# Decay parameters in five background parts, sample chain and triangular inverse paced by the weights, cache rows and stores issued by SyncE

## The chip, the cores and the metric

The kernel runs on one core of a Trainium2 chip. TensorE (PE) multiplies, VectorE (DVE), ScalarE (ACT) and GpSimd (POOL) work on whole tiles, SyncE (SP) only issues transfers. SP's transfers run on a hardware queue (q1 in the profile), GpSimd's on a software queue (q0); both are carried by the same 16 DMA engines. The metric is the device time of one launch in microseconds. Before the change it is 2061.14 us, the median of three runs (2057.72 to 2062.92).

## The reference, cut to what matters

One layer of a decoder for 256 prompt tokens and 8 × 4 sample tokens (288 columns together), model width 2048:

```
h = RMSNorm(x)
(GDN q|k|v|z|beta|alpha, attention q|k|v (3 groups x 4 heads), pool channels, 3 gates) = h @ w_in
A: gated DeltaNet: short conv, SiLU, L2-normed q/k, per-head decay; prompt in chunks with the
   inverse of (1 + lower); sample from its own state
   beta = sigmoid(ba);  g = -exp(a_log) * softplus(aa + dt_bias);  decays from cumsum(g)
B: dilated window attention, groups (128,1), (512,4), (2048,16); sample tokens also see the caches
C: pooled channels, linear map
x = x + RMSNorm(merge(A, B, C with gates) @ w_out)
x = x + RMSNorm(SwiGLU(RMSNorm(x)))
```

The outputs also hold the new cache windows, GDN states, conv and pool rows. All is float32; a product of x and w is made of three products of rounded parts (wh·xh, wh·xl, wl·xh).

## The kernel before

**The main stream.** Some 590 weight tiles of 512 KB are read in a fixed order, one after another, and never again. SP loads a tile (`raw`, L169, five buffers), ACT rounds it (`wh`, L180), DVE subtracts (`wl`, L184), three buffers each, and PE runs 24 matmuls of 288 columns on it (L253 to L255). `plan` puts the items of the layer in a list (w_in by its column blocks, then the branch weights, w_out, the gate and up weights, w_down); `run_items` walks through it. At the end of an item its sums are taken out of PSUM (evacuations, `ev`).

**Background work.** Everything else is written as Python generators. After each tile `step` (L282) advances every started generator by its rate: R_G for the two head groups of the GDN (3.8 and 3.45 steps a tile), R_S = 4.4 for the sample attention, R_P = 1 for the prompt attention. A bare `yield` ends one step, `yield n` passes n tiles. The instructions are then put on their engines by a scheduler that estimates times; each engine runs its own in that order. `paced` (L274) puts an instruction behind the last `wl` on DVE, so that this work can't run ahead of the weights.

**GDN.** `beta_alpha` (L414) computes beta, the decays and their sums (`egc`, `egl`, `egls`) once, all in one piece, when two rounds of tokens are through. `gdn` (L662) does the prompt: the inverse of a triangular matrix takes 31 steps of two DVE instructions, `tm` (L741) and `X` (L743). `gdn_sample` (L854) has a chain of small matmuls with an engine's answer between: `ys`, `zs`, `ws`, `avs` (L891 to L912).

**Sample attention.** `attn_sample` (L1077) reads the caches as 118 rows `kr` of 256 KB (128 partitions × 512 values), in five buffers (KR = 5), keys first and values after. Groups 1 and 2 give 2 × 48 rows by L1106, whose source is four of the group's positions, each for 32 places (8 sequences × 4 quarters), thus 4 × 32 × 512; group 0 gives 2 × 8 by L1111 (128 × 512) and a few come from a scratch copy of the new rows (`scr`, L1089, L1112). DVE multiplies keys with queries (`junk`, L1142) and values with scores (`ot`, L1192). All these are issued by GpSimd (`dq = nc.gpsimd`). So are the stores of the new rows (`nat`, copied by L979 and L981): `win_prompt` (L986), `scr` (L988), `win_sample` (L991). Tiles like `nat`, `pT`, `oah`, `ev` and the GDN's are slots of one list of 98 (`U`, L123), handed out in the order in which they were freed: whoever takes a slot waits for the transfer that last read it.

Of the kernel before, what the change touches and what calls it, by code (L numbers as in the profile page):

```python
# [9 lines left out]
F32 = mybir.dt.float32  # L10
F32R = mybir.dt.float32r
AF = mybir.ActivationFunctionType
OP = mybir.AluOpType
# [4 lines left out]
NT, NP, NS = 288, 256, 32  # L18
# [6 lines left out]
KR = 5  # L25
EPS = 1e-6
SC = 128.0 ** -0.5
WIN = (128, 512, 1028)
# [59 lines left out]

class Layer:
    COPY_FROM = 310  # L90
    R_G, R_S, R_P, R_R = (3.8, 3.45), 4.4, 1, 1.4

    def __init__(self, ctx, tc, a, o):
        self.ctx, self.tc, self.nc, self.a, self.o = ctx, tc, tc.nc, a, o
        P = self.pool
        self.cp = P("cp")
        self.raw_p = P("rawp", 5)
        self.wh_p = P("whp", 3)
        self.wl_p = P("wlp", 3)
        self.up = P("up")  # L100
        self.sm = P("sm", 2)
        self.dr = P("dr", space=DRAM)
        self.pm = P("pm", 4, space=PSUM)
        self.pb = P("pb", 4, space=PSUM)
        self.ufree = deque(range(NU))
        self.uslot = {}
        self.bg = []
        self.chained = {}
        self.tiles = deque()
        self.pend = deque()  # L110
        self.items = []
        self.n = 0
        self.paced_to = None
        self.raws = deque()
        self.hold = None
        self.out_a, self.out_b, self.out_c = {}, {}, {}
        self.dq = self.nc.gpsimd
# [153 lines left out]
            self.behind(ins, self.chained[key])  # L271
        self.chained[key] = ins

    def paced(self, ins):  # L274

        if self.paced_to is not self.last_wl:
            self.paced_to = self.last_wl
            self.behind(ins, self.last_wl)
        self.chain(ins)
        return ins  # L280

    def step(self):  # L282
# [131 lines left out]
    def beta_alpha(self):  # L414
# [6 lines left out]
        for k in range(4):  # L421
            for j in range(4):
                d = j * 4 + k
                nc.tensor.matmul(p[32 * j:32 * j + 32, :NT], lhsT=w[:, d * 16:d * 16 + 32], rhs=self.xT[d],
                                 start=k == 0, stop=k == 3, tile_position=(0, 32 * j))
        bat = w
        nc.vector.tensor_tensor(bat, p[:, :NT], self.r0, op=OP.mult)
        pt = self.ps("bat")
        for ch in range(2):
# [1 line left out]
                             start=True, stop=True)  # L431
        nc.tensor.matmul(pt[:16, 32:64], lhsT=c["gsel"], rhs=bat[:, NP:], start=True, stop=True)
        nc.vector.tensor_copy(bat[:16, NP:], pt[:16, 32:64])
        dba = self.dr.tile([16, 32], F32, name="dba")
        self.dq.dma_start(dba, bat[:16, NP:])
        beta = self.cp.tile([128, 2, 9], F32, name="beta")
# [29 lines left out]
        nc.vector.tensor_tensor(w1, w1, w2, op=OP.add)  # L466
        nc.vector.scalar_tensor_tensor(w1, z2, 0.0, w1, op0=OP.max, op1=OP.add)
        nc.vector.scalar_tensor_tensor(g, w1, -1.0, ex[:, 2], op0=OP.mult, op1=OP.mult)
        pc = self.ps("cum")
        for k, (lu, lub) in enumerate((("U", "Ub"), ("V", "Vb"), ("ones", None))):  # L470
            nc.tensor.matmul(pc[:, k * 32:k * 32 + 18], lhsT=c[lu], rhs=g, start=True, stop=True)
# [8 lines left out]
                nc.scalar.activation(dst[:, :, 8:9], v[:, :, 8:9], AF.Exp)  # L480
        self.beta, self.gl, self.egc, self.esf, self.egl = beta, g, egc, esf, egl
        self.egls = []
        pe = self.ps("egls")
        for hg in range(2):
            t = self.cp.tile([128, 32], F32, name=f"egls{hg}")
            nc.vector.tensor_scalar(t, c["bsel"], g[:, hg * 9 + 8:hg * 9 + 9], None, op0=OP.mult)
            nc.tensor.matmul(pe[:, hg * 32:hg * 32 + 32], lhsT=c["ones"], rhs=t, start=True, stop=True)
            t2 = self.cp.tile([128, 32], F32, name=f"eglx{hg}")
            nc.scalar.activation(t2, pe[:, hg * 32:hg * 32 + 32], AF.Exp)
            self.egls.append(t2)  # L490


    def mixer_plan(self):
# [20 lines left out]

        def second():
            self.drain(self.rms0)
            self.beta_alpha()
            self.resc = self.start(self.rescale(), self.R_R)

        def conv_mixed():  # L520
# [64 lines left out]
                          after=(lambda blks=blks, part=part: self.down_done(blks, part)) if n == 3 else None)  # L585

    def gdn_start(self, hg):
        self.G[hg]["gen"] = self.start(self.gdn(hg), self.R_G[hg])

    def gdn_finish(self):  # L590
# [71 lines left out]
    def gdn(self, hg):  # L662
# [75 lines left out]
        for j in range(31):  # L738
            n, m = 31 - j, j + 1
            tv = tm[:, :n * m].rearrange("p (a b) -> p a b", a=n)  # L740
            nc.vector.tensor_tensor(tv, lb[:, j, j + 1:, None].to_broadcast([32, n, m]),  # L741
                                    X[:, j:j + 1, :m].to_broadcast([32, n, m]), op=OP.mult)
            nc.vector.tensor_tensor(X[:, j + 1:, :m], X[:, j + 1:, :m], tv, op=OP.subtract)  # L743
            yield
        nc.vector.tensor_copy(lb, X.rearrange("p i c -> p c i"))
# [108 lines left out]
    def gdn_sample(self, hg, G, la, kn, bv, beta, egc, nbe, kdc, qsc):  # L854
        nc, c, pp = self.nc, self.c, self.pap
        X = 8
# [31 lines left out]
        p = self.ps("ys")  # L888
        nc.tensor.matmul(p[:, 0:128], lhsT=x1[:, 0:128], rhs=R, start=True, stop=True)
        nc.scalar.copy(T[:, 0:128], p[:, 0:128])  # L890
        yield  # L891
        p = self.ps("zs")
        nc.tensor.matmul(p[:, 0:128], lhsT=x1[:, 128:256], rhs=T[:, 0:128], start=True, stop=True)
        nc.vector.tensor_copy(T[:, 128:256], p[:, 0:128])
        yield
        p = self.ps("ws")
        nc.tensor.matmul(p[:, 0:128], lhsT=x1[:, 0:128], rhs=T[:, 128:256], start=True, stop=True)
        V = T[:, 0:128]
        nc.vector.tensor_tensor(V, V, p[:, 0:128], op=OP.subtract)
        self.free(x1)  # L900
        yield
        p = self.ps("avs")
        nc.tensor.matmul(p[:, 0:128], lhsT=la[:, 128:256], rhs=V, start=True, stop=True)
        o = self.U(name="os")
        nc.vector.tensor_tensor(o[:, 0:128], qs, p[:, 0:128], op=OP.add)
        so = self.small(1, "sos")
        nc.scalar.activation(o[:, 128:256], o[:, 0:128], AF.Square, scale=qsc[:, X:X + 1], accum_out=so)
        nc.scalar.activation(so, so, AF.Sqrt, bias=self.eps, scale=1.0 / 128)
        nc.vector.reciprocal(so, so)
        nc.vector.tensor_tensor(so, so, qsc[:, X:X + 1], op=OP.mult)  # L910
        nc.scalar.activation(o[:, 0:128], o[:, 0:128], AF.Copy, scale=so)
        yield  # L912

        kd = kn[:, 0:128]
        nc.gpsimd.tensor_scalar(kd, kd, kdc[:, X:X + 1], None, op0=OP.mult)
# [39 lines left out]
    def evac_qkv(self, kind, g):  # L955
        vT = []

        def evac(h, ps):
            nc = self.nc
            t = self.res.popleft()  # L960
            nc.scalar.copy(t, ps)
            if kind == 2:
                vT.append(t)
            else:
                (self.kT if kind == 1 else self.qT)[g, h] = t
            if h < 3:
                return
            src = vT if kind == 2 else [(self.kT if kind == 1 else self.qT)[g, j] for j in range(4)]
            for tb in ([2] if kind == 0 else [1, 2] if (kind == 1 and g == 0) else [0, 1, 2]):
                w = NS if tb == 2 else 128  # L970
                p = self.ps("knat")
                for j in range(4):
                    nc.tensor.transpose(p[:w, j * 128:j * 128 + 128], src[j][:, tb * 128:tb * 128 + w],
                                        self.c["ident"])
                for hp in range(2):
                    n = self.U(name="nat")
                    cs = slice(hp * 256, hp * 256 + 256)
                    if hp == 0:
                        nc.scalar.copy(n[:w, :256], p[:w, cs])  # L979
                    else:  # L980
                        nc.vector.tensor_copy(n[:w, :256], p[:w, cs])  # L981
                    if tb < 2:
                        if not (g == 0 and tb == 0):
                            o = self.o[f"win{g + 1}_prompt"][0, 0].rearrange("r k h d -> r k (h d)")
                            r0 = 0 if g == 0 else tb * 128
                            self.dq.dma_start(o[r0:r0 + 128, kind - 1, cs], n[:, :256])  # L986
                    else:
                        self.dq.dma_start(self.scr[kind, g][:, cs], n[:NS, :256])  # L988
                        if kind > 0:
                            o = self.o[f"win{g + 1}_sample"][0].rearrange("b r k h d -> b r k (h d)")  # L990
                            self.dq.dma_start(o[:, WIN[g] - 4:, kind - 1, cs], n[:NS, :256])  # L991
                    if kind == 2 and tb < 2:
                        self.vn[g, tb, hp] = n
                    else:
                        self.free(n)
            self.free(*vT)
        evac.res = 4
        return evac
# [78 lines left out]
    def attn_sample(self, pool):  # L1077
# [8 lines left out]
        def by_t(dst, kind, g):  # L1086
            src = scr[kind, g].rearrange("(b t) d -> t b d", t=4)
            for t in range(4):
                dq.dma_start(dst[t * 32:t * 32 + 32], src[t][:, None, :].to_broadcast([8, 4, 512]))  # L1089

        for g in (1, 2):
            by_t(qt[:, g - 1], 0, g)
        q0s = scr[0, 0].rearrange("(b t) d -> t b d", t=4)
        for t in range(4):
            dq.dma_start(big[:, t], q0s[t][:, None, :].to_broadcast([8, 16, 512]))
        cw = [a["cache_win1"][0], a["cache_win2"][0], a["cache_win3"][0]]

        def row():
# [2 lines left out]
        def sources(kv):  # L1101

            for g, dil, n in ((1, 4, 32), (2, 16, 16)):
                src = cw[g].rearrange("b (q m r) k h d -> m k r (b q) (h d)", q=4, r=dil)
                for m in range(n):
                    yield g, (m if g == 1 else 32 + m), lambda kr, s=src[m, kv][:4]: dq.dma_start(kr, s)  # L1106
            for g in (1, 2):
                yield g, 47 + g, lambda kr, g=g: by_t(kr, 1 + kv, g)
            src = cw[0].rearrange("b (s m) k h d -> m k (b s) (h d)", m=8)
            for m in range(8):  # L1110
                yield 0, m, lambda kr, s=src[m, kv]: dq.dma_start(kr, s)  # L1111
            yield 0, 8, lambda kr: dq.dma_start(kr, scr[1 + kv, 0][:, None, :].to_broadcast([32, 4, 512]))  # L1112

        todo = deque((kv,) + r for kv in range(2) for r in sources(kv))
        got = deque()
# [13 lines left out]
                if not got:  # L1129
                    return  # L1130

        for _ in range(KR - 1):
            load()
        yield 5

# [385 lines left out]
```

## Time and profile before

| | |
|---|---|
| median of three runs | 2061.14 us |
| the profiled execution, its own time | 2068.37 us |
| its span | 2066.6 us |
| mean granted clock of TensorE | 0.992 |
| read and written in device memory | 410.44 MB, 66.63 MB |

Rows that name an engine give busy microseconds, then its share of the span. A row "A <- B: t, n, m" says that A waited for B t us in total, n times, m at most. Stretches (windows) give for each engine the busy time in a piece of the span, the granted clock (PEclk), the DMA share (1.00: all 16 engines busy) and GB/s. Queue rows give packets, megabytes and the share of 16 engines; transfer rows the count, the KB of one and the median time from issue to landing.

### The profile page before, as it was taken

The numbers are of one execution on the slowest core, as the hardware profiler recorded it, in microseconds if no ns is written. First come the engines' busy times: TensorE is split into PE (matmuls) and PEld (weight loads), VectorE is DVE, ScalarE is ACT, GpSimd is POOL, SyncE is SP. The second block draws the span as 40 slices with busy tenths as digits, with TensorE's granted clock in tenths as the row PEclk, the third lists the DMA queues.
The fourth block names the chain that finished last, engine by engine and source line by source line (L and its number), as shares of the span: only waits on it lengthen the run. The fifth ranks groups of instructions, "written<-read, shape, count | busy, mean of one in ns | idle before, by whom it ended". The sixth has DMA issues, their size and how long they took to land. (4 is left out here: it accounts for less than half of the span.)

```text
span 2066.6 us, 38707 instructions
## 1 busy us (share of the span) xinstructions
PE 2010.6 (97%) x15212; PEld 1984.4 (96%) x15212; DVE 1324.2 (64%) x2857; ACT 893.8 (43%) x1414; POOL 291.6 (14%) x504
## 2 busy tenths in 40 slices
PE   8999999999799999989999989999999999999998
PEld 8989998999799999989999989999999999999997
DVE  7969558567688779878875475543554445454555
ACT  6654473453344444333334454334333333333344
POOL 2326312523320022322000000000000000000001
PEclk9999999999999999999999989999999999999999
DMA  8565546959995668998677646766767767677662
GB/s 268 160 182 169 176 140 197 228 173 238 219 205 183 181 184 198 226 220 245 195 229 234 218 160 212 226 222 217 225 216 228 230 217 226 218 225 227 217 205 97
DMA packets 240310, 425.50 MB, mean 206 GB/s; under 512 B 42736, under 2 KB 83200, under 8 KB 238464
## 3 DMA queue, kind: packets, MB, share of 16 engines
q1 hardware_dynamic: 207712, 384.72, 63.1%
q0 software_dynamic: 32272, 37.73, 8.0%
q8 instruction: 119, 1.95, 0.4%
q10 hardware_dynamic: 144, 0.59, 0.1%
q14 instruction: 63, 0.52, 0.1%
HBM read 410.44 MB, written 66.63 MB: 231 GB/s over the span
## 5 line engine op out<-in xcount | busy, mean ns | idle before, releaser
L184 DVE TENSOR_TENSOR wl<-raw,wh 128x1024 fp32r<-128x1024 f32 x585 | 720.2, 1232 | 519.0 <-ACT wh L180 516.7
L180 ACT CAST wh<-raw 128x1024 fp32r<-128x1024 f32 x585 | 612.7, 1050 | 917.9 <-PE m L254 792.3
L253 PE MATMUL m<-hh,wh 128*128 128x288 f32 x1792 | 532.7, 299 | 4.2 <-ACT wh L180 3.7
L255 PE MATMUL m<-hh,wl 128*128 128x288 f32 x1792 | 524.0, 298 | 8.3 <-DVE wl L184 8.3
L254 PE MATMUL m<-hl,wh 128*128 128x288 f32 x1792 | 531.3, 298 | 0.0
L253 PE MATMUL m<-xgh,wh 128*128 128x288 f32 x1408 | 415.8, 297 | 4.0 <-ACT xgh L373 4.0
L254 PE MATMUL m<-xgl,wh 128*128 128x288 f32 x1408 | 415.8, 296 | 3.2 <-DVE xgl L374 3.2
L255 PE MATMUL m<-xgh,wl 128*128 128x288 f32 x1408 | 414.6, 296 | 0.0
L255 PEld LDWEIGHTS m<-hh,wl 128*128 128x128 f32 x1792 | 335.1, 189 | 13.1 <-DVE wl L184 10.7
L253 PEld LDWEIGHTS m<-hh,wh 128*128 128x128 f32 x1792 | 337.7, 189 | 7.8 <-ACT wh L180 4.2
L254 PEld LDWEIGHTS m<-hl,wh 128*128 128x128 f32 x1792 | 338.2, 189 | 1.9 <-issue 1.8
L253 PEld LDWEIGHTS m<-xgh,wh 128*128 128x128 f32 x1408 | 265.5, 189 | 4.6 <-ACT xgh L373 4.3
L254 PEld LDWEIGHTS m<-xgl,wh 128*128 128x128 f32 x1408 | 266.4, 189 | 3.6 <-DVE xgl L374 3.5
L255 PEld LDWEIGHTS m<-xgh,wl 128*128 128x128 f32 x1408 | 265.4, 189 | 0.0
L253 PE MATMUL m<-hidh,wh 128*128 128x288 f32 x704 | 207.5, 295 | 0.0
L254 PE MATMUL m<-hidl,wh 128*128 128x288 f32 x704 | 207.2, 295 | 0.0
L255 PE MATMUL m<-hidh,wl 128*128 128x288 f32 x704 | 206.5, 295 | 0.0
L1449 POOL TENSOR_TENSOR yo<-y,xr 128x288 f32<-128x288 f32 x7 | 5.6, 821 | 1060.7 <-DVE y L1440 1060.7
L254 PEld LDWEIGHTS m<-hidl,wh 128*128 128x128 f32 x704 | 132.4, 188 | 0.0
L253 PEld LDWEIGHTS m<-hidh,wh 128*128 128x128 f32 x704 | 132.2, 188 | 0.0
L255 PEld LDWEIGHTS m<-hidh,wl 128*128 128x128 f32 x704 | 131.9, 188 | 0.0
L1106 POOL DMA_DIRECT2D kr<-cache_win x96 | 65.4, 682 | 250.0 <-DVE junk L1142 136.9
(386 smaller groups left out, 2704.4 us busy)
## 6 DMA issues: line engine op xcount, KB each, us to landing
raw<-w_in SPq DMA_DIRECT2D x247, 512.0 KB, 4.5
raw<-w_gu SPq DMA_DIRECT2D x176, 512.0 KB, 4.0
raw<-w_down SPq DMA_DIRECT2D x88, 512.0 KB, 4.9
win_sample<-cache_win SPq DMA_DIRECT2D x64, 512.0 KB, 5.4
kr<-cache_win POOLq DMA_DIRECT2D x112, 256.0 KB, 10.7
raw<-w_out SPq DMA_DIRECT2D x32, 512.0 KB, 5.0
win_sample<-cache_win SPq DMA_DIRECT2D x32, 508.0 KB, 5.2
st<-state_gdn SPq DMA_DIRECT2D x64, 128.0 KB, 3.2
```

What stands on the lines that cost most here:

```text
L180: i = nc.scalar.copy(wh, raw)
L184: self.last_wl = nc.vector.tensor_tensor(wl, raw, wh.bitcast(F32), op=OP.subtract)
L253: nc.tensor.matmul(out, lhsT=wh[:, c], rhs=xh, start=k == 0, stop=False)
L254: nc.tensor.matmul(out, lhsT=wh[:, c], rhs=xl, start=False, stop=False)
L255: nc.tensor.matmul(out, lhsT=wl[:, c], rhs=xh, start=False, stop=k == nk - 1)
L1106: yield g, (m if g == 1 else 32 + m), lambda kr, s=src[m, kv][:4]: dq.dma_start(kr, s)
L1449: (nc.vector if how == "v" else nc.gpsimd).tensor_tensor(out[:, d % 2], y, x, op=OP.add)
```

## The change

Four edits go together.

1. `beta_alpha` becomes a generator with four `yield`s (five parts), started at 0.6 steps a tile and drained in `gdn_start`; the two products for `egls` are made ahead of the last part. R_G rises from (3.8, 3.45) to (4.3, 3.9).
2. The links of the sample chain are `yield 1` instead of `yield`; one more `yield` stands ahead of its square root.
3. The first instruction of each step of the inverse is `paced` by the weights, with a chain of its own (key "x").
4. All cache rows, their scratch rows and the stores of new rows are issued by `nc.sync`; three rows are loaded ahead of the first use instead of four.

```diff
-    R_G, R_S, R_P, R_R = (3.8, 3.45), 4.4, 1, 1.4
+    R_G, R_S, R_P, R_R = (4.3, 3.9), 4.4, 1, 1.4
...
-    def paced(self, ins):
-
-        if self.paced_to is not self.last_wl:
-            self.paced_to = self.last_wl
+    def paced(self, ins, key="sample"):
+
+        if self.paced_to.get(key) is not self.last_wl:
+            self.paced_to[key] = self.last_wl
             self.behind(ins, self.last_wl)
-        self.chain(ins)
+        self.chain(ins, key)
...
         bat = w
+        yield
...
         nc.vector.tensor_copy(bat[:16, NP:], pt[:16, 32:64])
+        yield
...
+        yield
         pc = self.ps("cum")
...
+        ts = [self.cp.tile([128, 32], F32, name=f"egls{hg}") for hg in range(2)]
+        for hg in range(2):
+            nc.vector.tensor_scalar(ts[hg], c["bsel"], g[:, hg * 9 + 8:hg * 9 + 9], None, op0=OP.mult)
+        yield
...
-            self.beta_alpha()
+            self.ba = self.start(self.beta_alpha(), 0.6)
...
     def gdn_start(self, hg):
+        self.drain(self.ba)
...
-            nc.vector.tensor_tensor(tv, lb[:, j, j + 1:, None].to_broadcast([32, n, m]),
-                                    X[:, j:j + 1, :m].to_broadcast([32, n, m]), op=OP.mult)
+            self.paced(nc.vector.tensor_tensor(tv, lb[:, j, j + 1:, None].to_broadcast([32, n, m]),
+                                               X[:, j:j + 1, :m].to_broadcast([32, n, m]), op=OP.mult), "x")
...
         nc.scalar.copy(T[:, 0:128], p[:, 0:128])
-        yield
+        yield 1
...
-                            self.dq.dma_start(o[r0:r0 + 128, kind - 1, cs], n[:, :256])
+                            nc.sync.dma_start(o[r0:r0 + 128, kind - 1, cs], n[:, :256])
...
-                        self.dq.dma_start(self.scr[kind, g][:, cs], n[:NS, :256])
+                        nc.sync.dma_start(self.scr[kind, g][:, cs], n[:NS, :256])
...
-                            self.dq.dma_start(o[:, WIN[g] - 4:, kind - 1, cs], n[:NS, :256])
+                            nc.sync.dma_start(o[:, WIN[g] - 4:, kind - 1, cs], n[:NS, :256])
...
-                dq.dma_start(dst[t * 32:t * 32 + 32], src[t][:, None, :].to_broadcast([8, 4, 512]))
+                nc.sync.dma_start(dst[t * 32:t * 32 + 32], src[t][:, None, :].to_broadcast([8, 4, 512]))
...
                 src = cw[g].rearrange("b (q m r) k h d -> m k r (b q) (h d)", q=4, r=dil)
                 for m in range(n):
-                    yield g, (m if g == 1 else 32 + m), lambda kr, s=src[m, kv][:4]: dq.dma_start(kr, s)
+                    yield g, (m if g == 1 else 32 + m), lambda kr, s=src[m, kv][:4]: nc.sync.dma_start(kr, s)
...
-                yield 0, m, lambda kr, s=src[m, kv]: dq.dma_start(kr, s)
+                yield 0, m, lambda kr, s=src[m, kv]: nc.sync.dma_start(kr, s)
...
-        for _ in range(KR - 1):
+        for _ in range(KR - 2):
             load()
```

How it moves the instructions, at three places. First, the middle of the sample attention's keys, where the new rows of group 1 are stored. GpSimd's queue before held cache rows, then stores (`nat_650` to `nat_657`), then rows again, and SP's queue beside it nothing but `raw`:

```order
L1106 DMA kr_6875<-cache_win2 128x1x512
L1106 DMA kr_6919<-cache_win2 128x1x512
L986 DMA win2_prompt<-nat_650_6843 128x256
L986 DMA win2_prompt<-nat_653_6854 128x256
L988 DMA scr_109<-nat_656_6865 32x256
L991 DMA win2_sample<-nat_656_6865 8x4x256
```

SP's queue after the change, at the same stores:

```order
L1114 DMA kr_6953<-cache_win2 128x1x512
L994 DMA win2_prompt<-nat_650_6841 128x256
L994 DMA win2_prompt<-nat_653_6852 128x256
L994 DMA win2_prompt<-nat_651_6844 128x256
L994 DMA win2_prompt<-nat_654_6855 128x256
L996 DMA scr_109<-nat_656_6863 32x256
L999 DMA win2_sample<-nat_656_6863 8x4x256
L996 DMA scr_109<-nat_657_6867 32x256
L999 DMA win2_sample<-nat_657_6867 8x4x256
L1114 DMA kr_6989<-cache_win2 128x1x512
L169 DMA raw_7106<-w_in 128x2x512
L169 DMA raw_7142<-w_in 128x2x512
```

Rows and weights now take turns in one queue, with eight stores in a row between them. Second, ACT at the change of items in the middle of w_in (near 420 us in the trace of before), with the semaphores that each instruction waits for (DMAHW is SP's queue, DMASW GpSimd's). Before:

```order
L795 COPY y_582_5540<-y_583_5541 128x128 [waits DMASW6_49,DMASW5_49,PE_49]
L961 COPY ev_570_5438<-m_5442 128x288 [waits DMASW7_49,PE_49]
L787 ACTIVATE S_575_5479<-ks_580_5530,egc_803 128x128 [waits DMASW2_49,DVE_49]
L961 COPY ev_571_5439<-m_5443 128x288 [waits PE_49,Pool_49]
L787 ACTIVATE S_577_5486<-ks_581_5535,egc_803 128x128 [waits DMASW4_49,DMASW3_49,DVE_49]
L961 COPY ev_572_5440<-m_5444 128x288 [waits PE_49]
```

After:

```order
L987 COPY nat_579_5465<-knat_578_5460 128x256 [waits PE_49,Pool_49]
L987 COPY nat_582_5476<-knat_581_5471 32x256 [waits PE_49]
L802 COPY y_584_5484<-y_585_5485 128x128 [waits PE_49]
L969 COPY ev_590_5498<-m_5502 128x288 [waits DMAHW0_49,Activation_49]
L969 COPY ev_591_5499<-m_5503 128x288 [waits DMAHW5_49,DMAHW2_49,DVE_49]
L969 COPY ev_592_5500<-m_5504 128x288 [waits DMAHW4_49,DMAHW3_49,Activation_49]
```

Three evacuations in a row now take slots whose last reader is the store of a `nat` copied a few instructions ahead. Third, DVE in the first inverse. Before, a piece between two `wl`:

```order
L184 TENSOR_TENSOR wl<-raw,wh 128x1024
L741 TENSOR_TENSOR tm<-lb,X 32x156
L894 COPY ys_1972<-zs_2020 128x128
L743 TENSOR_TENSOR X<-X,tm 32x26x6
L741 TENSOR_TENSOR tm<-lb,X 32x175
L743 TENSOR_TENSOR X<-X,tm 32x25x7
L741 TENSOR_TENSOR tm<-lb,X 32x192
L184 TENSOR_TENSOR wl<-raw,wh 128x1024
```

After, the same steps:

```order
L748 TENSOR_TENSOR tm<-lb,X 32x156
L926 TENSOR_SCALAR vz_2037<-ys_1938,cc 128x128
L750 TENSOR_TENSOR X<-X,tm 32x26x6
L926 TENSOR_SCALAR vz_2038<-ys_1938,cc 128x128
L748 TENSOR_TENSOR tm<-lb,X 32x175
```

The steps of the inverse stand three tiles later, among the products that follow the sample chain, where before they still stood beside the chain itself.

More of the change, by code (lines that the diff above doesn't have):

```diff
@@ L112, in __init__ @@
         self.n = 0
-        self.paced_to = None
+        self.paced_to = {}
         self.raws = deque()
@@ L482, in beta_alpha @@
         self.egls = []
+        ts = [self.cp.tile([128, 32], F32, name=f"egls{hg}") for hg in range(2)]
+        for hg in range(2):
+            nc.vector.tensor_scalar(ts[hg], c["bsel"], g[:, hg * 9 + 8:hg * 9 + 9], None, op0=OP.mult)
+        yield
         pe = self.ps("egls")
         for hg in range(2):
-            t = self.cp.tile([128, 32], F32, name=f"egls{hg}")
-            nc.vector.tensor_scalar(t, c["bsel"], g[:, hg * 9 + 8:hg * 9 + 9], None, op0=OP.mult)
+            t = ts[hg]
             nc.tensor.matmul(pe[:, hg * 32:hg * 32 + 32], lhsT=c["ones"], rhs=t, start=True, stop=True)
@@ L894, in gdn_sample @@
         nc.vector.tensor_copy(T[:, 128:256], p[:, 0:128])
-        yield
+        yield 1
         p = self.ps("ws")
@@ L900, in gdn_sample @@
         self.free(x1)
-        yield
+        yield 1
         p = self.ps("avs")
@@ L907, in gdn_sample @@
         nc.scalar.activation(o[:, 128:256], o[:, 0:128], AF.Square, scale=qsc[:, X:X + 1], accum_out=so)
+        yield
         nc.scalar.activation(so, so, AF.Sqrt, bias=self.eps, scale=1.0 / 128)
@@ L911, in gdn_sample @@
         nc.scalar.activation(o[:, 0:128], o[:, 0:128], AF.Copy, scale=so)
-        yield
+        yield 1
         kd = kn[:, 0:128]
@@ L1094, in attn_sample @@
         for t in range(4):
-            dq.dma_start(big[:, t], q0s[t][:, None, :].to_broadcast([8, 16, 512]))
+            nc.sync.dma_start(big[:, t], q0s[t][:, None, :].to_broadcast([8, 16, 512]))
         cw = [a["cache_win1"][0], a["cache_win2"][0], a["cache_win3"][0]]
@@ L1110, in sources @@
             for m in range(8):
-                yield 0, m, lambda kr, s=src[m, kv]: dq.dma_start(kr, s)
-            yield 0, 8, lambda kr: dq.dma_start(kr, scr[1 + kv, 0][:, None, :].to_broadcast([32, 4, 512]))
+                yield 0, m, lambda kr, s=src[m, kv]: nc.sync.dma_start(kr, s)
+            yield 0, 8, lambda kr: nc.sync.dma_start(kr, scr[1 + kv, 0][:, None, :].to_broadcast([32, 4, 512]))
         todo = deque((kv,) + r for kv in range(2) for r in sources(kv))
```

## The prediction

> **What bounds the kernel now.** I read the busy shares first, then the span cut into stretches, then who waited for whom inside the bad stretches, then the DMA lists there. The page says that the matmul engine sets the time:
>
> ```profile
> span 2066.6 us, 38707 instructions
> ...
> PE 2010.6 (97%) x15212; PEld 1984.4 (96%) x15212; DVE 1324.2 (64%) x2857; ACT 893.8 (43%) x1414; POOL 291.6 (14%) x504
> ```
>
> TensorE is idle for 2066.6 − 2010.6 = 56 us, so no change that only removes waits gains more than that (plus some clock). The stretches say where:
>
> ```profile
> core 0: us, PE busy (x) PEld busy (x) DVE busy (x) ACT busy (x) POOL busy (x), PEclk, DMA share, GB/s
> 100.00:150.00 50.00, 46.10 (x443) 44.60 (x442) 32.09 (x91) 31.49 (x92) 12.19 (x24) 1.00 0.63 180
> ...
> 500.00:560.00 60.00, 53.79 (x402) 52.31 (x401) 40.38 (x156) 23.34 (x37) 19.42 (x32) 1.00 1.01 221
> 560.00:600.00 40.00, 33.19 (x237) 32.79 (x235) 27.42 (x102) 17.67 (x28) 8.60 (x13) 0.91 0.95 195
> ...
> 800.00:850.00 50.00, 49.50 (x370) 48.96 (x370) 44.19 (x94) 22.14 (x30) 14.37 (x19) 1.00 1.02 213
> 850.00:950.00 100.00, 90.96 (x663) 89.36 (x662) 77.08 (x154) 33.33 (x40) 29.21 (x44) 0.98 1.07 234
> ```
>
> Sample attention with cache rows loses 6.2 + 6.8 us (500 to 600) and 0.5 + 9.0 us (800 to 950): 22.5 of the 56, and only there does the DMA share stand at 1. Who waits, first over the whole span (PE), then DVE for 480 to 560 and 850 to 950, and ACT for 480 to 560:
>
> ```profile
> PE m L255 <- DVE wl L184: 14.7, 12, 2.8
> PE pv L1065 <- ACT pT L1057: 6.8, 1, 6.8
> PE egls L487 <- ACT eglx L489: 1.4, 1, 1.4
> PE ws L897 <- DVE ys L894: 1.2, 1, 1.2
> ```
> ```profile
> DVE junk L1142 <- DMA kr<-cache_win: 15.0, 8, 4.8
> DVE ot L1192 <- DMA kr<-cache_win: 18.4, 12, 4.2
> ACT oah L146 <- DMA win_sample<-nat: 9.2, 1, 9.2
> ```
>
> DVE works in order: while it waits for a cache row `kr`, the next `wl` stands behind the waiting instruction, and PE runs dry. One such event:
>
> ```profile
> 912.40 0.35 DVE L1192 SCALAR_TENSOR_TENSOR ot<-kr,sct,ot 128x128 f32<-128x128 f32 x1 [4.16 <-DMA kr<-cache_win]
> 912.67 1.22 DVE L184 TENSOR_TENSOR wl<-raw,wh 128x1024 fp32r<-128x1024 f32 x1
> ...
> 913.95 0.40 PE L255 MATMUL m<-och,wl 128*128 128x288 f32 x1 [2.76 <-DVE wl L184]
> ```
>
> ACT's 9.2 us is a slot held by a store that stands on GpSimd's queue behind rows. So both losses begin with late transfers, and the change moves just these.
>
> **The cache rows, the large term.** How long a row needs: the first two lines below are the landing times of the rows of groups 1 and 2 (L1106, 96 of them) and of group 0 (L1111, 16), both 256 KB on GpSimd's queue; the third is that queue from 458 to 460 us, while one row of L1106 is moving.
>
> ```profile
> DMA to landing us min/median/max: 5.1/11.6/20.9
> DMA to landing us min/median/max: 3.0/4.6/7.2
> q0 software_dynamic: 63, 0.19, 25.5%
> ```
>
> One row of L1106 keeps 25.5% of 16 engines busy, that is four. Its source has four rows as its outermost dimension (`[:4]`, then 32 cache places), L1111's has 128; that is what makes 5.1 us the best of the one and 3.0 of the other. Four engines carry 0.19 MB in 2 us, 23.3 GB/s each. On GpSimd's queue the fours change: a row uses a quarter, and the share over the whole stretch below is full.
>
> After the change the same 96 transfers, with the same shape, go out on SyncE's queue. **Which four engines they get there decides the time**, and no row shows it: every transfer that this queue issued before has an outermost dimension of 16, 32 or 128. I take the case that it is always the same four; the other end, that they change or that all sixteen are used, is rival 1. This is a choice between ends far apart. [...]
>
> The price. What one engine carries per microsecond on the hardware queue, in a burst of weights (645 to 645.75) and over a long quiet stretch (1400 to 1500), and what both queues together carry where they mix (460 to 600):
>
> ```profile
> DMA packets 135, 0.28 MB, mean 369 GB/s; under 512 B 0, under 2 KB 0, under 8 KB 135
> q1 hardware_dynamic: 135, 0.28, 100.2%
> ```
> ```profile
> DMA packets 8806, 22.17 MB, mean 222 GB/s; under 512 B 671, under 2 KB 671, under 8 KB 8621
> q1 hardware_dynamic: 8797, 22.05, 69.9%
> ```
> ```profile
> DMA packets 20786, 30.46 MB, mean 218 GB/s; under 512 B 8966, under 2 KB 8966, under 8 KB 20773
> q1 hardware_dynamic: 9268, 17.87, 58.0%
> q0 software_dynamic: 11505, 12.43, 40.8%
> ...
> raw<-w_in SPq DMA_DIRECT2D x31, 512.0 KB, 10.2
> kr<-cache_win POOLq DMA_DIRECT2D x39, 256.0 KB, 10.1
> raw<-w_br_a SPq DMA_DIRECT2D x4, 512.0 KB, 9.2
> ```
>
> That is 369 / 16 = 23.1 GB/s, 222 / (16 × 0.70) = 19.8, and 218 / (16 × 0.988) = 13.8. I take 19.8, the long row with the hardware queue alone, and keep the others as ends. A row puts 65.5 KB on each of its four engines: 3.31 us. A weight tile puts 32.8 KB on each of 16: 1.66 us. Between 460 and 600 the four engines would have 39 × 3.31 + 35 × 1.66 = 187 us of work where 140 us passed: **+47**. For 800 to 950 (q1's megabytes over 0.524 give 43 tiles):
>
> ```profile
> q1 hardware_dynamic: 11705, 22.50, 67.6%
> ...
> kr<-cache_win POOLq DMA_DIRECT2D x43, 256.0 KB, 12.8
> ```
>
> 43 × 3.31 + 43 × 1.66 = 214 us where 150 passed: **+64**. Of the other 14 rows five are loaded long before their use; nine at the same 111 / 82 = 1.35 us give **+12**. Together +123 us. The idle time and slow clock of these stretches is swallowed: the windows counted include it. The wait lands on DVE at L1150 and L1200 for `kr`, on ACT for `raw`, and through both on PE. At 23.1 GB/s the same sums give 160 and 182 us, +20, +32 and +6: +58. At 16 GB/s they are 232 and 265, +92, +115 and +23: +230; 13.8 would need all sixteen engines loaded, and here twelve are not, so I stop at 16. The clock can add to it: a matmul is 2010.6 / 15212 = 0.132 us, a tile of 24 is 3.2 us, and at half clock throughout it would be 6.3 against the 187 / 35 = 5.3 us of a tile, +78 in all; the 0.91 above, after a stall of 6.8 us, shows a small part of that, so I add nothing and leave it to the range.
>
> **Issuing.** GpSimd loses 112 cache rows and 50 stores (and 30 small loads of the new rows), SyncE gains them:
>
> ```profile
> L1106 POOL DMA_DIRECT2D kr<-cache_win x96 | 65.4, 682 | 250.0 <-DVE junk L1142 136.9
> ...
> 509.44 0.37 SPq L169 DMA_DIRECT2D raw<-w_in  x1
> ```
>
> At 0.37 us and about two transfers a tile SyncE is far from full; between 0.37 and 0.68 us for a row it makes no bound. But raws now queue behind rows that wait for DVE, and share the completion slots with them: that is rival 3.
>
> **The background parts.** The parameters in five parts keep the second `egls` matmul as close behind its ACT partner as it was, and the sample chain's links stood about a tile apart already; at most the 1.4 and 1.2 us above, twice for the latter kind, are won, so 0 to −4, taken 0. The inverse: paced by the weights, its steps start three tiles later. Two steps of wl:
>
> ```profile
> 157.91 1.20 DVE L184 TENSOR_TENSOR wl<-raw,wh 128x1024 fp32r<-128x1024 f32 x1
> ...
> 163.89 1.21 DVE L184 TENSOR_TENSOR wl<-raw,wh 128x1024 fp32r<-128x1024 f32 x1
> ```
>
> With 6.0 us between two `wl` DVE is already overfull there and the three buffers just bear it. By the order the work between wl's is lumped in two tiles instead of three, with the same sum; from 0 to +3, taken +1, and the faster rates R_G only pay for the added yields. At the change of items near 420 us the order shows three evacuations (L969) on ACT that wait for stores just issued:
>
> ```profile
> gdn_sample<-st SPq DMA_DIRECT2D x32, 128.0 KB, 3.3
> ```
>
> At 3.3 us a store, and PE having up to three tiles of other work, 0 to +4, taken +1. Sum of all: +123 + 0 + 1 + 1 = **+125 us**. On the profiled execution that is 2066.6 + 125 = 2192 of span, 2193 of its own 2068.37; this run lies 7 us above the median 2061.14, so I say 2061 + 125 = **2186 us**.
>
> **Rivals.** (1) *The fours change on SyncE's queue too, or all engines share a row.* Then rows and weights run in one ring at 19.8 GB/s × 16 = 317 GB/s, where a tile and 1.1 rows need 0.81 MB, 2.6 us, less than a tile's time; landings fall toward what a raw has where few rows run (640 to 740):
>
> ```profile
> raw<-w_in SPq DMA_DIRECT2D x21, 512.0 KB, 3.7
> ```
>
> The 13.0 + 9.5 us idle shrink to some 5.5, the clock gives back about 3: −20 + 2 = −18, about 2043 (2034 to 2055). For it: the waits named all start with late rows. Chance 0.20. (2) *The transfers share the engines as before and land as late:* between +2 and half of rival 1, 2052 to 2065, within 0.3% (about what a measurement of this kernel can tell from no change). [...] Chance 0.07. (3) *Only the queue's order hurts:* no hot engines, but landings stay near 10 us, and with eight transfers in flight and three a tile where eight stores go out in a row, a tile takes 3 × 10.2 / 8 = 3.8 us instead of 3.2, some 26 tiles: +16, with a few waits of raws behind rows +25, 2086. It decides from landings of some 8.5 us up. Chance 0.03.
>
> **The numbers.** The same four engines 0.70, rivals 0.20, 0.07, 0.03. Forecast's own range 2119 to 2290. Of it some 0.1 lies above 2265; to hold 8 in 10 the range must reach down to rival 1, so 2038 to 2265. Faster 0.20, same 0.07, slower 0.73.
>
> **What would show it.** If right: rows of L1114 land in 15 us or more and raws of the attention stretches no faster than now, while the mean DMA share of these stretches falls well under 1 (four engines full, twelve at about a third: near 0.5); DVE's waits for `kr` or ACT's for `raw` grow to tens of microseconds; PE is under 75% busy from 460 to 650 and again in the value half; the rows of group 0 (L1119) land quickly. If `kr` lands in 4 to 6 us and the share stays above 0.75, rival 1 holds. GDN wrong: PE idle between 130 and 430 us changes by over 5 us.

## The result, and the profile after

The changed kernel takes **2153.08 us** (median of four runs, 2149.44 to 2156.81) against 2062.03 for the kernel before in the same comparison: ratio **1.0444**, 95% interval 1.0418 to 1.0469, so 91 us slower. The forecast was 2186, +125 us. Its profiled execution has a span of 2151.3 us, 84.7 more than that of before. The page:

```profile
span 2151.3 us, 38669 instructions
...
PE 2033.2 (95%) x15212; PEld 1998.4 (93%) x15212; DVE 1327.4 (62%) x2857; ACT 889.4 (41%) x1413; POOL 174.9 (8%) x312
```

PE's idle time grew by 62.1 us, from 56.0 to 118.1, and the same 15212 matmuls are busy 22.6 us longer, while the granted clock fell (mean 0.980 against 0.992). 62.1 + 22.6 are the 84.7 us. Where: the two pieces in which the rows of groups 1 and 2 are used, from the first product with such a row to the last, keys and then values. Before:

```profile
core 0: us, PE busy (x) PEld busy (x) DVE busy (x) ACT busy (x) POOL busy (x), PEclk, DMA share, GB/s
451.40:628.00 176.60, 163.57 (x1220) 161.45 (x1219) 129.82 (x496) 70.95 (x108) 54.07 (x89) 0.98 0.99 225
778.60:951.20 172.60, 162.09 (x1190) 159.48 (x1189) 143.26 (x302) 64.90 (x83) 50.39 (x77) 0.99 1.01 223
```

After, the same work:

```profile
460.80:677.90 217.10, 173.77 (x1230) 169.31 (x1228) 128.92 (x498) 70.25 (x110) 0.00 (x0) 0.91 0.59 173
827.70:1034.80 207.10, 169.40 (x1170) 163.26 (x1169) 142.38 (x301) 62.54 (x81) 15.94 (x23) 0.94 0.60 178
```

The keys took 40.5 us longer, the values 34.5; the first piece began 9.4 us later, and these three sum to 84.4. The 9.4 us come up with "The size" below. Between the two and behind them the time is the same within 1 us. The telling column is the DMA share: the pieces wait for transfers, DVE for `kr` and ACT for `raw` (below, over the whole span), and yet the sixteen engines are busy for 0.6 of the time, where they were full before. The waits after:

```profile
DVE junk L1150 <- DMA kr<-cache_win: 52.5, 29, 5.3
DVE ot L1200 <- DMA kr<-cache_win: 49.7, 29, 5.0
```
```profile
ACT wh L180 <- DMA raw<-w_in: 111.4, 37, 10.4
```

The same waits before:

```profile
DVE junk L1142 <- DMA kr<-cache_win: 15.0, 8, 4.8
DVE ot L1192 <- DMA kr<-cache_win: 21.8, 16, 4.2
```
```profile
ACT wh L180 <- DMA raw<-w_in: 22.0, 10, 3.3
```

That fits a few full engines beside many waiting ones. Counted in the trace's packet records, exactly four data packets of SyncE's queue (512 B and more) were under way at 36% of the moments between 470 and 640 us; the next most frequent number, 16, came to 13%.

If all rows ride the same four engines, each of these carried in the keys 43 rows of 65.5 KB, four rows of group 0 (16.4 KB, taken as spread over all sixteen: up to 14 packets of a lone one were under way at once in the trace of before, 629.5 to 633 us) and 44 tiles of 32.8 KB: 4325 KB in 217.1 us, 19.9 GB/s. In the values 42 rows, four of group 0, 47 full tiles and 4 half ones in 207.1 us are 21.4. The small stores are not counted. The counts are these (keys):

```profile
q1 hardware_dynamic: 21146, 37.32, 58.1%
...
raw<-w_in SPq DMA_DIRECT2D x36, 512.0 KB
kr<-cache_win SPq DMA_DIRECT2D x47, 256.0 KB
raw<-w_br_a SPq DMA_DIRECT2D x8, 512.0 KB
```
```profile
L1114 SPq DMA_DIRECT2D kr<-cache_win x43: 547/1190/3971, 467.6 to 656.8; - x43
L1119 SPq DMA_DIRECT2D kr<-cache_win x4: 389/620/1042, 672.9 to 677.1; - x4
```

### The profile page after: what moved, and what is told of

Read it like the earlier page. It is cut to its first block, busy times and chain, and to the rows that moved or that the text cites. A ratio compares the mean times of both kernels' runs of the same rounds, so it can differ in the third digit from the quotient of the medians.

```text
span 2151.3 us, 38669 instructions
## 1 busy us (share of the span) xinstructions
PE 2033.2 (95%) x15212; PEld 1998.4 (93%) x15212; DVE 1327.4 (62%) x2857; ACT 889.4 (41%) x1413; POOL 174.9 (8%) x312
## 5 line engine op out<-in xcount | busy, mean ns | idle before, releaser
L253 PEld LDWEIGHTS m<-hh,wh 128*128 128x128 f32 x1792 | 341.2, 191 | 16.4 <-ACT wh L180 11.1
L254 PE MATMUL m<-hidl,wh 128*128 128x288 f32 x704 | 207.1, 294 | 0.0
L1200 DVE SCALAR_TENSOR_TENSOR ot<-kr,sct,ot 128x128 f32<-128x128 f32 x196 | 70.1, 358 | 53.9 <-DMA kr<-cache_win 49.7
```

What stands on the lines that cost most here:

```text
L253: nc.tensor.matmul(out, lhsT=wh[:, c], rhs=xh, start=k == 0, stop=False)
L254: nc.tensor.matmul(out, lhsT=wh[:, c], rhs=xl, start=False, stop=False)
L1200: self.paced(e.scalar_tensor_tensor(dst, kr[:, hs], pr, dst, op0=OP.mult, op1=OP.add))
```

## The experiments

Theory **H**: a row of groups 1 and 2, 4 × 32 × 512, rides four engines, on SyncE's queue always the same four. Theory **Q**: the loss is the queue's order: rows, stores and weights in one line, waits at its head, shared completion slots. Theory **G**: it is the background edits.

| run | what it is | median us | ratio to before (95%) |
|---|---|---|---|
| e1_spread16 | changed kernel, places of a row reordered | 2043.32 | 0.9894 (0.9869 to 0.9920) |
| e2_rows_back | changed kernel, row loads on GpSimd | 2072.10 | 1.0032 (1.0015 to 1.0049) |
| e3_only_rows | before, the 96 rows on SyncE | 2154.11 | 1.0434 (1.0402 to 1.0466) |
| e4_background | before, background edits alone | 2071.22 | 1.0036 (1.0019 to 1.0054) |
| e6_two_engines | changed kernel, a row in halves of 2 × 32 × 512 | 2370.14 | 1.1485 (1.1450 to 1.1521) |
| e5_four_parts | changed kernel, a row in four transfers of 32 × 512 | 2056.73 | 0.9971 (0.9959 to 0.9984) |
| e7_spread_sync_alone | before, queue edits with reordered places | 2038.48 | 0.9878 (0.9859 to 0.9898) |
| e8_spread_gpsimd | before, reordered places alone | 2037.38 | 0.9877 (0.9852 to 0.9902) |
| e8b_spread_gpsimd | the same once more | 2038.00 | 0.9879 (0.9860 to 0.9898) |
| e9_spread_parts_chain | e8 with parts, rates, sample chain | 2043.43 | 0.9906 (0.9888 to 0.9925) |
| e10_spread_paced_x | e8 with the paced inverse | 2044.04 | 0.9909 (0.9889 to 0.9929) |

The kernel before had medians of 2064.12 us beside the first four, 2062.80 beside the next four and 2062.25 beside the last three.

**The places of a row in another order.** Partitions of a row run over (sequence, quarter, token) instead of (token, sequence, quarter). The transfer then has 32 as its outermost dimension; two small masks, the maxima's layout and the query's copies follow.

```diff
-                src = cw[g].rearrange("b (q m r) k h d -> m k r (b q) (h d)", q=4, r=dil)
+                src = cw[g].rearrange("b (q m r) k h d -> m k (b q) r (h d)", q=4, r=dil)
...
-                    ... lambda kr, s=src[m, kv][:4]: nc.sync.dma_start(kr, s)
+                    ... lambda kr, s=src[m, kv][:, :4]: nc.sync.dma_start(kr, s)
...
-    d["sel1"] = (t // 32 == c % 4) & ((t % 32) // 4 == c // 4)
+    d["sel1"] = (t % 4 == c % 4) & (t // 16 == c // 4)
...
-    mt[:, 48:] = t % 4 == 0
+    mt[:, 48:] = t // 4 % 4 == 0
```

> The changed kernel with the 128 places of a row of groups 1 and 2 put in another order, (sequence, quarter, token) instead of (token, sequence, quarter), so that the source of a row is 32 x 4 x 512 and no longer 4 x 32 x 512; queue, order, count and size of the transfers stay. Theory H (same four engines on SyncE's queue): the row spreads over 16 engines, the time falls by 90 to 110 us to 2040 to 2060, PE idle between 450 and 1050 us under 15 us, and waits of DVE for kr nearly gone. Theory Q (rows, stores and weights in one queue, waits at its head, shared completion slots): within 15 us of 2153. Theory G (the background edits): within 15 us of 2153.

2043.32 us: 110 us faster than the changed kernel and 1.1% faster than before, in the same queue, with the same number and size of cache-row transfers (only the rows and query copies from the scratch come in eight pieces instead of four). DVE has no wait for `kr` left, and PE idles 3.6 us between 450 and 1050. The two bad pieces, in stretches of the same run:

```profile
451.00:651.00 200.00, 200.00 (x1531) 199.28 (x1530) 164.85 (x616) 93.56 (x148) 1.08 (x2) 1.00 0.73 231
800.00:1000.00 200.00, 199.51 (x1506) 199.04 (x1505) 178.79 (x360) 74.27 (x87) 14.98 (x16) 1.00 0.74 232
```

PE is full at full clock, 231 GB/s instead of 173. Q and G fall as causes of the loss.

**Row loads back on GpSimd.**

```diff
-                    ... lambda kr, s=src[m, kv][:4]: nc.sync.dma_start(kr, s)
+                    ... lambda kr, s=src[m, kv][:4]: dq.dma_start(kr, s)
```

(and the same for L1097, L1103, L1119, L1120)

> The changed kernel with all row loads (and their scratch rows) back on GpSimd's queue; stores stay on SyncE, background edits stay, three rows ahead. H: 2050 to 2066, rows land in 8 to 13 us as before, and the waits of DVE for kr return to some 30 us. Q: the stores between the weights still cost, 2075 or more. G: about 2150.

2072.10: the loss goes with the rows, but the time is a little above H's 2066. The rows land in 11.2 us (median), and DVE waits 20.8 us for them, less than the 30 expected. The time equals that of the background edits alone (1.0032 against 1.0036), so the fifty stores on SyncE cost nothing that shows.

**Only the 96 rows on SyncE, all else as before.**

```diff
-                    ... lambda kr, s=src[m, kv][:4]: dq.dma_start(kr, s)
+                    ... lambda kr, s=src[m, kv][:4]: nc.sync.dma_start(kr, s)
```

> The kernel before with nothing changed but the 96 rows of groups 1 and 2, which SyncE issues. H: the whole loss comes from these, 2125 to 2165. Q: the stores and small loads are not in the queue, so half of the loss at most, under 2110. G: about 2062.

2154.11: this one line brings the whole loss. In the profiled run 6 us of it come only behind the last matmul (see "Background edits" below).

**The background edits alone** (all transfers issued as before).

> The three background edits alone (parameters in five parts with the new rates, sample chain, paced inverse), all transfers as before. H and Q: 2058 to 2068, since the forecast put them at +2. G: over 2080.

2071.22, +7 (4 to 11 by the interval), above what H and Q expected. In this run the stalls at `egls` and `ws` (106 and 149 us before) are gone, and new ones stand behind it. PE's waits between 100 and 400 us, then one of the whole span, which lies between 390 and 460, and what ACT waited for ahead of it:

```profile
PE ded L773 <- POOL dd L764: 3.4, 2, 2.8
PE ot L851 <- ACT bv L847: 1.6, 1, 1.6
```
```profile
PE zz L807 <- ACT y L802: 3.6, 1, 3.6
```
```profile
ACT y L802 <- DMA scr<-nat: 6.1, 1, 6.1
```

**The dose: two engines a row.**

```diff
-                    ... nc.sync.dma_start(kr, s)
+                    ... [nc.sync.dma_start(kr[r * 64:r * 64 + 64], s[2 * r:2 * r + 2]) for r in range(2)]
```

> The changed kernel with each row of groups 1 and 2 loaded as two transfers of 2 x 32 x 512. H: each half rides two engines, the same two, so a row puts 131 KB on each. In the changed kernel's profile four engines carried 33 rows and 30 weight tiles in 150 us (3.15 MB each, 21.0 GB/s); at that rate a row costs 6.2 us and a tile 1.56, the sums of the prediction give 39 x 6.2 + 35 x 1.56 = 296 for 140 us and 43 x 6.2 + 43 x 1.56 = 334 for 150, nine more rows some 37: about +377, and 2440 us with the background edits (2390 to 2500). Q, if only the number of transfers in the queue counts: one more a row, some +20 to +60, 2170 to 2215.

2370.14: far over what Q allows, and 70 below H's number, 20 below its range. The mean DMA share falls again, and the clock with it:

```profile
500.00:800.00 300.00, 184.38 (x1086) 174.34 (x1087) 119.19 (x457) 67.10 (x105) 0.54 (x1) 0.78 0.39 124
```

Here exactly two packets were under way at 58% of the moments from 500 to 780 us. In the 300 us 80 halves and 45 tiles (37 of w_in, 8 of w_br_a) put 80 × 65.5 + 45 × 32.8 = 6716 KB on each of the two engines, 22.4 GB/s, more than the 21.0 expected. With that rate (5.85 us a row, 1.46 a tile) and the rows counted rightly (four of the 43 are of group 0, see "The size" below), the two stretches give +139 and +144 us, in sum 283. From the first product with such a row to the last, keys and values took 144 and 136 us longer than before; another 19 us were lost ahead of the keys. So H's price was somewhat too high and its count as well.

**Four transfers a row**, each of 32 × 512.

```diff
-                    ... nc.sync.dma_start(kr, s)
+                    ... [nc.sync.dma_start(kr[r * 32:r * 32 + 32], s[r]) for r in range(4)]
```

> The changed kernel with each row of groups 1 and 2 loaded as four transfers of 32 x 512, one for each token. H: each spreads over 16 engines, the hot four are gone, 2040 to 2075, although SyncE issues 288 transfers more and a row takes four completion slots. Q: more transfers in the queue make it worse than 2153.

2056.73: with four times as many row transfers in the same queue, 96 us faster than the changed kernel; the places keep their order, the transfers differ in shape. The additional transfers have their price too: 13 us more than e1, most of it in the keys (PE 171.04 of 180 us busy from 460 to 640, where e1 is full).

**The queue edits without the background edits, places reordered.**

> The kernel before with the queue edits alone (rows, scratch rows and stores on SyncE, three rows ahead) and the places of a row ordered as in the first run; no background edits. H with the background edits at +7: 2043 - 7 = 2036 (2030 to 2042). If the background edits cost nothing once the rows are quick: 2043 within 3.

2038.48, inside the first answer; against e1's 2043.32 the intervals overlap.

**Places reordered, everything still on GpSimd's queue.** The kernel before with the diff of e1, `dq` in place of `nc.sync`.

> The kernel before with only the places of a row reordered; everything stays on GpSimd's queue. If the late rows of before were also due to four engines a row: 2040 to 2050. If they were due to two queues that share the engines (the forecast's rival 1 needs SyncE): 2058 to 2066.

2037.38, again 2038.00, a little under the first answer's 2040. So the late rows of before were due to the four engines a row as well, and with rows that spread, the queue makes no difference (2037 and 2038 against 2038). The landing times of the rows of L1106, before and here (min, median, max):

```profile
DMA to landing us min/median/max: 5.1/11.6/20.9
```
```profile
DMA to landing us min/median/max: 2.8/4.0/9.5
```

**Parts, rates and chain; and the paced inverse, each upon e8.**

> The kernel of e8 once more, as the base of the next two on the same chip: 2037, within 4.

> The kernel of e8 with the parameters in five parts, the new rates R_G and the sample chain a tile per link, without the paced inverse. The background edits together cost about 7 us where they stood alone. If the rates and chain cost it: 2041 to 2047. If the paced inverse does: 2033 to 2038, since the waits of 1.4 and 1.2 us near 120 us go away.

> The kernel of e8 with the paced inverse alone. If it costs the 7 us: 2041 to 2047, with the loss between 130 and 260 us. If the rates and chain do: 2035 to 2040.

2043.43 and 2044.04 against 2038.00: each costs some 5 to 6 us by the medians, so each meets the answer that blames it. The two do not add up: both together cost 5 where the rows are quick (e1 against e7). The intervals of the ratios overlap those of e8, so the size is not settled. The paced inverse does what it says where DVE was overfull, and gives it back behind. PE busy in the base (e8b):

```profile
130.00:200.00 70.00, 66.65 (x576) 62.20 (x575) 62.04 (x170) 26.33 (x47) 31.04 (x49) 1.00 0.65 187
200.00:260.00 60.00, 58.01 (x447) 57.43 (x446) 37.92 (x72) 29.35 (x66) 15.96 (x40) 1.00 0.53 161
```

And with the paced inverse (e10):

```profile
130.00:200.00 70.00, 70.00 (x603) 66.23 (x603) 60.36 (x156) 29.05 (x56) 38.59 (x54) 1.00 0.66 192
200.00:260.00 60.00, 55.93 (x390) 54.47 (x389) 37.79 (x75) 23.25 (x45) 16.35 (x35) 0.91 0.53 155
```

3.35 us won from 130 to 200, 2.08 lost from 200 to 260, where the clock also falls to 0.91, up to 0.09 × 60 = 5.4 us more.

## Why the prediction was right

**Bound and place.** It said that cache rows set the time in two stretches, and that one of two things would happen there. It was the first: the same four engines. Shown by e3 (one line, the whole loss), e1 and e5 (same queue, other shape, no loss) and e6 (half as many engines, +307 us instead of +91).

**The choice.** The prediction called the four engines on SyncE a choice between far ends. No row of before told which; the 0.70 on the same four was its author's estimate. The runs show the number of engines on this queue: with rows of four, four packets at a time and 0.59 share; with halves of two, two packets and 0.39. The completions go the same way: in the kernel before 851 transfers on the hardware queues leave 13616 increments of semaphores in the trace, 16 each; with the 96 rows among them (e3) 947 leave 14096, five for a row. In e6 a half leaves three, in e5 a part 16. Why it is five and three, one more than the packets under way, no trace explains. That the four are always the same follows from the rate: 19.9 and 21.4 GB/s for each of four is near the 23.1 of a burst, and more engines would share the load. Which of the sixteen they are is not shown, since the trace does not number them.

**The size.** +125 was forecast, +91 measured. Three terms were mis-sized. The first is the price of a row: 19.8 GB/s an engine, from a stretch whose engines were 70% busy, where 33 rows and 30 tiles in the 150 us from 500 to 650 of the changed kernel, 3.15 MB on each engine, make 21.0. The second is a count: four of the 43 rows between 800 and 950 are of group 0 (L1111), counted here as spread over all sixteen engines (up to 14 packets of one at once, above). At 21.0 and with 39 rows the prediction's two sums give 39 × 3.12 + 35 × 1.56 = 176 and 39 × 3.12 + 4 × 0.78 + 43 × 1.56 = 192, so +36 and +42, 78 in place of 111; the two pieces took 75 us longer. The other end of the range, 23.1, would have been as near.

The third is the rest. The prediction put +12 on nine rows outside the stretches and nothing on the five loaded long before their use. No time is lost between the pieces; the five cost some 10 us. Here is what PE and then ACT wait for between 390 and 462 us in e3, which has no background edits; the kernel before has none of these waits there:

```profile
PE zz L800 <- ACT y L795: 5.0, 1, 5.0
PE ded L766 <- ACT e L764: 2.4, 1, 2.4
```
```profile
ACT wh L180 <- DMA raw<-w_in: 13.7, 2, 7.6
```

The first five rows go out between weight tiles from 382 us on, ACT waits twice for a tile, and what PE needs from ACT (`e`, `y`) stands behind. The first product with a row comes at 461.6 us, 10.2 later than before. In the changed kernel it comes 9.4 later, with one such wait of 7.0 us; how much of that the background edits cause is not separated.

**The clock.** "I add nothing" holds for the sum, but not because the clock kept up: with 0.91 and 0.94 in the two pieces PE was busy 10.2 and 7.3 us longer for about the same work. PE waits for transfers there anyway, so this probably lies inside their time; no run separates it. A lower mean alone is no loss here: the profiled run of e7 records 0.944, nearly all of it an even 0.949, and PE is busy 2007.3 us, as in e1 (2007.8 at 0.994).

**Issuing.** That SyncE "is far from full" at 0.37 to 0.68 us was wrong as it stood. A row of L1114 took it, min, median, max in ns, after the change and with spread places (e1):

```profile
L1114 SPq DMA_DIRECT2D kr<-cache_win x96: 536/1191/4538, 390.1 to 1014.3; - x96
```
```profile
L1114 SPq DMA_DIRECT2D kr<-cache_win x96: 534/541/1447, 393.4 to 904.7; - x96
```

With rows on four engines, issuing itself waits, 1191 ns against 541 in the median. That it adds no loss of its own is likely, since 19.9 and 21.4 GB/s on each of the four are near the 23.1 of a burst, but was not separated.

**Background edits.** Forecast +2 (−4 to +7 by its bounds), measured +7 alone, some 5 to 6 for each half and 5 for both on the quick rows. The chain's waits of 1.4 and 1.2 us went, as said; the step that failed is that only DVE's lumps and ACT's store waits were priced. The new waits are of PE for GpSimd (`dd`) and for ACT (`bv`, `y`), each a few microseconds, with the clock behind them. In the changed kernel they seem to add little to the rows' loss: e3 without them is as slow (1.0434 against 1.0444). But in the profiled runs e3 is 7.3 us ahead at its last copy on ACT (L1447 at 2139.5 us, L1455 of the changed kernel at 2146.8) and then takes 10.8 us to its end instead of 4.5; why is open. The predicted wait of evacuations for stores near 420 us is there (ACT, 400 to 450 us of the changed kernel):

```profile
ACT ev L969 <- DMA scr<-nat: 2.5, 1, 2.5
```

but in e1 ACT waits 2.7 us there too while PE is full from 400 to 450, so it need not cost anything; with the stores still on GpSimd (e4) it was 6.1 us in front of `y`, and PE lost 3.6.

**The rivals.** Rival 1's price was right to the microsecond, 2043 against 2043.32 in e1, which is the case it describes, but by luck: the quick rows alone gain 25 us (e8), not 20, and the background edits cost some 5, not 2. Its reason was half wrong: it took the mixing of two queues for what slowed the rows before, and e8 shows rows landing in 4.0 us on the second queue once they spread. Rival 2 (the same landings, 2052 to 2065) did not come. Rival 3's mechanism is at most small: +13 in e5 with four times the row transfers.

**What would show it** said: PE under 75% from 460 to 650 and again in the values; it was 79% (149.71 of 190), and 82% from 827.7 to 1034.8. Waits of tens of microseconds and a share well under 1 came as said. The landing times that it names are not in the profile of SyncE's queue. Its sign for the GDN, over 5 us more PE idle between 130 and 430, came out at 4.6 in the changed kernel and 6.0 in e4.

## What to carry to other kernels

Here the rows kept their shape when they moved to another queue, and the DMA share of the keys fell from 0.99 to 0.59: look at the outermost dimension of the source first, and when it is small, reorder the data before asking which queue is better. With 4 and 2 four and two packets were under way; with 32 a row landed in 4.0 us instead of 11.6 (e8), and the queue made no difference any more (2038.48 against 2037.38). A mean DMA share of 0.59 and 0.39 beside waits for transfers of 102 us and more (DVE for `kr`) meant four and two full engines here, as many as that dimension. The reorder alone, with nothing else of the change, gives the fastest kernel measured: 2037.38 us, 1.2% under the kernel before (ratio 0.9877, 0.9852 to 0.9902).

## What the runs showed of the hardware that was not expected

Four-engine rows hurt on the software queue as well, where they cannot always be the same four, since one row keeps 25.5% of the engines busy and the share of the keys is 0.99: 11.6 us to landing against 4.0 for the reordered rows (e8), and the weights' transfers beside them landed in 10.2 us against 4.5 (e8, 460 to 600 us), though a row and a tile have the same bytes and the DMA share of that stretch fell from 0.99 to 0.80 while the rate rose from 218 to 246 GB/s:

```profile
DMA packets 15895, 34.51 MB, mean 246 GB/s; under 512 B 2324, under 2 KB 2324, under 8 KB 15881
...
raw<-w_in SPq DMA_DIRECT2D x32, 512.0 KB, 4.5
kr<-cache_win POOLq DMA_DIRECT2D x41, 256.0 KB, 4.2
```

Why the same bytes then keep the engines busy for less time is not settled. The packets under 512 B in this stretch fell from 8966 to 2324, but all of them took only 112 of the 2217 us of packet time before. It is the large ones that got quicker: a weight's packet of 2 KB from 140 to 84 ns (median), a packet of 4 KB on GpSimd's queue from 271 to 159.
